# Sums into the output of a Strassen product: from VectorE to ScalarE and an accumulating DMA, with one half of two operand sums emitted two tiles earlier

## The chip, the cores and the metric

The kernel runs on one core of one Trainium2 chip. The metric is the time of one execution on the device in microseconds (us). The core has five engines that work at once, each on its own list of instructions: TensorE (PE; its weight loads are a row of their own, PEld), VectorE (DVE), ScalarE (ACT), GpSimd (POOL) and SyncE (SP). SyncE and GpSimd issue most DMA transfers here. SBUF is the working memory on the chip, PSUM the memory that TensorE writes its results to, DRAM the large memory outside.

## The reference

A decoder trunk of two layers over 512 tokens of width 1024, in float32. Each layer is a mixing part with three attention-like branches, and then a squared-ReLU MLP. The change lies in the MLP alone:

```python
h = rmsnorm(x, norm_mlp_g[l])
x = x + jnp.square(jax.nn.relu(h @ w_up[l])) @ w_down[l]   # w_up 1024 x 4096, w_down 4096 x 1024
```

A last RMSNorm closes the trunk.

## The kernel before, in words

**Number format.** Every float32 operand of a large matmul is split into two parts, `hi` (a ScalarE copy to the matmul's format) and `lo` (what is left, a VectorE subtraction); three matmuls, hi x hi, hi x lo and lo x hi, make one product. `split_to` (L573, L574) does it for activations, `Weights.split` (L159/L160 and L171) for weights, some tiles ahead of their use: four pairs of buffers `whi`/`wlo` stand in a ring, and the code splits two units ahead. The code adds weight blocks for Strassen on VectorE (L438) or by loads whose second DMA adds to the first in SBUF (L123, issued by GpSimd).

**The MLP of a layer.** The 4096 hidden columns are taken in four groups of 1024 (`g` = 0 to 3). For each group eight "up" tiles are computed (`tile_T`, L586 to L588: 24 matmuls of 128 x 512 each). For `g` = 0, 1, 2 the product with `w_down` is one level of Strassen (`strassen()`): hidden and weight matrices are cut 2 x 2, and seven products P1 to P7 take the place of eight. The group `g` = 3 uses the plain product.

**One Strassen product.** `put_h` squares the ReLU of an up tile into the blocks H[t, i, q] (L1500, L1503): t is the half of the tokens, i the half of the hidden columns, q = 0, 1 a tile of 128 x 512 of it. The operands are blocks or sums of blocks: S1 = H11 - H10 (L1531), S2 = S1 - H00 up to sign (L1532), S4 (L1540), and H00 - H10 for P7 (L1525). `split_part` makes the hi and lo of an operand, for q = 0 and 1. `ready_early` makes P1's and P7's operands after the fourth up tile, `ready_sums` S1, S2 and P6's operand after the eighth.

The seven products run in the order P1, P7, P6, P4, P5, P2, P3 (`product`, L1564 to L1566: 24 matmuls each). They sum up in three pairs of PSUM banks: P1, P6, P5, P3 in "B"; P7, P4 in "D"; P2 in "A". After each product its bank's running sum is added to one block of the output (`add_to`), scaled by the token's factor, in tiles `acc[2i + t, j]` in SBUF: eight tiles, 128 x 512 each, that live through `g` = 0, 1, 2. The first sum into a tile is a scaled ScalarE copy (L1584), the others a VectorE instruction that reads PSUM and the tile (L1586):

```python
acc[key] = get()
nc.scalar.activation(acc[key], ps, AF.Copy, scale=r)
...
nc.vector.scalar_tensor_tensor(
    acc[key], in0=ps, scalar=r, in1=acc[key], op0=ALU.mult, op1=ALU.add
)
```

The next product in the same bank, and whoever gets the bank after `give`, has to wait until these have read it. In `g` = 3 `fold` transposes the eight tiles on TensorE (L1642) and adds them to the residual (L1643); the first fold comes with the first up tile of `g` = 3.

**Slots.** Activations, operands and sums share a ring of 42 SBUF tiles of 128 x 512: `get` takes the next free one, `put` gives one back to the end of the line. Whoever writes a slot next waits for its last reader.

**What sets the order.** Work behind a product (sums, splits) is put on a list with `defer` and emitted as soon as the count of emitted TensorE time reaches it, in the order of the calls; `need` and the wait for a free bank emit from that list at once. The order of emission is a priority: a planner (`schedule_with_timeline_sim=True`) then writes each engine's list of instructions, with its own estimates of their times, and takes what it holds to be ready. On the chip each engine follows its list in order. GpSimd's list holds the paired weight loads of the Strassen products (L123), the reload of x (L1377) and its store (L1452).

Of the kernel before, what the change touches and what calls it, by code (L numbers as in the profile page):

```python
# [13 lines left out]
AF = mybir.ActivationFunctionType  # L14
ALU = mybir.AluOpType
# [33 lines left out]
class Weights:  # L49
# [33 lines left out]
    def block(self, kind, srcs):  # L83

        c = len(self.chunks)
        self.chunks.append((srcs, 4, 512))
        self.left.append(None)
        self.queues[kind].append(c)
        return c
# [130 lines left out]
def trunk_kernel(  # L220
# [15 lines left out]
    nc = tc.nc  # L236
# [12 lines left out]
    def get(dtype=F32):  # L249
        i = slots.popleft()  # L250
        t = sb.tile([P, 512], dtype, name=f"slot{i}", tag=f"slot{i}")
        owner[id(t)] = (i, t)
        return t

    def get2():
        return get(R), get(R)

    def put(*ts):
        for t in ts:
            slots.append(owner.pop(id(t))[0])  # L260
# [64 lines left out]
    def defer(fn, delay=0):  # L325
        later.append((clock["t"] + delay, fn))
# [243 lines left out]
    def split_to(hi, lo, src, g=None):  # L570

        if g is None:
            nc.scalar.copy(hi, src)  # L573
            nc.vector.tensor_sub(lo, src, hi.bitcast(F32))  # L574
        else:
            nc.scalar.activation(hi, src, AF.Copy, scale=g)
            nc.vector.scalar_tensor_tensor(lo, in0=src, scalar=g, in1=hi.bitcast(F32), op0=ALU.mult, op1=ALU.subtract)  # L577
# [457 lines left out]
    def layer(l, box):  # L1035
# [381 lines left out]
        scale = {}  # L1417
# [68 lines left out]
        acc = {}  # L1486

        def strassen():

            H, parts = {}, {}  # L1490
# [14 lines left out]

                return go

            def split_part(name, src, free=True):
                got = parts[name] = []
                for q in range(2):  # L1510
                    hi, lo = get2()
                    split_to(hi, lo, src[q])
                    got.append((hi, lo))
                if free:
                    put(*src)

            def block(t, i):
                return [H[t, i, q] for q in range(2)]

            def ready_early():  # L1520

                split_part("P1", block(0, 0), False)
                s = [get() for _ in range(2)]
                for q in range(2):
                    nc.vector.tensor_sub(s[q], H[0, 0, q], H[1, 0, q])  # L1525
                split_part("P7", s)

            def ready_sums():

                for q in range(2):  # L1530
                    nc.vector.tensor_sub(H[1, 0, q], H[1, 1, q], H[1, 0, q])  # L1531
                    nc.vector.scalar_tensor_tensor(  # L1532
                        H[0, 0, q], in0=H[1, 0, q], scalar=-1.0, in1=H[0, 0, q], op0=ALU.mult, op1=ALU.subtract
                    )
                split_part("P6", block(0, 0), False)

            def ready_s4():

# [35 lines left out]
            def add_to(bank, i, j, sign):  # L1574


                def go():
                    for t in range(2):
                        ps = banks[bank][t]
                        r = scale[sign][:, 2 * i + t : 2 * i + t + 1]  # L1580
                        key = (2 * i + t, j)
                        if key not in acc:
                            acc[key] = get()
                            nc.scalar.activation(acc[key], ps, AF.Copy, scale=r)  # L1584
                        else:
                            nc.vector.scalar_tensor_tensor(  # L1586
                                acc[key], in0=ps, scalar=r, in1=acc[key], op0=ALU.mult, op1=ALU.add
                            )

                return go  # L1590

# [6 lines left out]
            for m in range(KD):  # L1598
                yield from tile_T(X, put_h(m))
                if m == 3:  # L1600
                    defer(ready_early)
            defer(ready_sums)
            need("P1", parts)
            yield from product("P1", "B", True, False)
            defer(add_to("B", 0, 0, "+"))
            yield from product("P7", "D", True, False)
            defer(add_to("D", 1, 1, "-"))
            defer(lambda: split_part("P4", block(1, 1)))
            need("P6", parts)
            yield from product("P6", "B", False, False)  # L1610
            defer(add_to("B", 1, 0, "+"))
            defer(lambda: split_part("P5", block(1, 0)))
            need("P4", parts)
            yield from product("P4", "D", False, True)
            defer(add_to("D", 1, 0, "+"))
# [13 lines left out]
            defer(give("B"))  # L1629

        def need(name, parts):
            while name not in parts:
                later.popleft()[1]()

        def fold(m):
# [13 lines left out]
        for g in range(4):  # L1649
            if g < 3:  # L1650
                if g == 2 and l < DEPTH - 1:
                    W.retired.extend(hold["pairs"])
                yield from strassen()
                continue
            for m in range(KD):
                defer(fold(m), 3000 + 4000 * m)
            if l < DEPTH - 1:
                W.retired.append(hold["wide"])
            for m in range(KD):
                yield from tile_T(X, put_up(m))  # L1660
            if (l, g) == (DEPTH - 1, 3):
                for hf in range(2):
                    c = slice(hf * 256, hf * 256 + 256)
                    for m in range(KD):
                        yield from tile_T(Later(hid, KD, c), put_last(m, c))
                    defer(lambda c=c: output(c))
                return
            for m in range(KD):
                yield from tile_T(Later(hid, KD), put_down(m, g == 3))

            def free_h(hs):
                for hi, lo in hs:
                    put(hi, lo)

            hs = [hid.pop(k) for k in range(KD)]
            defer(lambda hs=hs: free_h(hs))
# [80 lines left out]
```

## Time and profile before

| | us |
|---|---|
| three runs | 1826.11 (median), 1825.91, 1828.45 |
| the profiled execution, as timed | 1826.87 |
| its span, first to last instruction | 1825.1 |
| TensorE busy in the span | 1796.6 |
| VectorE busy | 1137.5 |
| ScalarE busy | 806.3 |
| GpSimd busy | 90.9 |

The span is what the trace covers; the time of an execution is 1.8 us longer here. Matmuls are pipelined, so a matmul's row lasts longer than the distance to the next. The lines that the table and the next section are from count times from the start of the span.

### The profile page before, as it was taken

The numbers are of one execution on the slowest core, as the hardware profiler recorded it, in microseconds if no ns is written. First come the engines' busy times: TensorE is split into PE (matmuls) and PEld (weight loads), VectorE is DVE, ScalarE is ACT, GpSimd is POOL, SyncE is SP. The second block draws the span as 40 slices with busy tenths as digits, with TensorE's granted clock in tenths as the row PEclk, the third lists the DMA queues.
The fourth block names the chain that finished last, engine by engine and source line by source line (L and its number), as shares of the span: only waits on it lengthen the run. The fifth ranks groups of instructions, "written<-read, shape, count | busy, mean of one in ns | idle before, by whom it ended". The sixth has DMA issues, their size and how long they took to land.

```text
span 1825.1 us, 22137 instructions
## 1 busy us (share of the span) xinstructions
PE 1796.6 (98%) x8848; PEld 1470.8 (81%) x8848; DVE 1137.5 (62%) x1746; ACT 806.3 (44%) x1359; POOL 90.9 (5%) x105
## 2 busy tenths in 40 slices
PE   7999999999999999999999999999999999999998
PEld 6877777788888887878898777778888888878787
DVE  6785765477454747475648657645765547475756
ACT  5654543133344644443446455422333346445344
POOL 1000000011000101000000000000110001010000
PEclk9999999999999999999999999999999999999999
DMA  6220122135423363623423112222344326362223
GB/s 210 81 93 25 60 93 81 58 95 149 149 92 106 98 179 93 181 65 101 133 78 104 47 37 83 71 92 69 104 139 150 93 92 160 117 163 91 93 93 116
DMA packets 150311, 188.59 MB, mean 103 GB/s; under 512 B 6592, under 2 KB 119760, under 8 KB 150208
## 3 DMA queue, kind: packets, MB, share of 16 engines
q1 hardware_dynamic: 137712, 154.68, 26.5%
q0 software_dynamic: 12352, 32.47, 7.2%
q8 instruction: 69, 1.13, 0.3%
q14 instruction: 34, 0.28, 0.0%
q10 hardware_dynamic: 144, 0.03, 0.0%
HBM read 182.97 MB, written 4.19 MB: 103 GB/s over the span
## 4 chain that ended last, share of the span: by engine, by line
PE 95%; DVE 3%; DMA 1%; ACT 1%; issue 0%; POOLq 0%; SPq 0%; DVEq 0%
PE d L586 12%; PE d L588 12%; PE d L587 12%; PE z L586 8%; PE z L587 8%; PE z L588 8%; PE d L658 3%; PE d L660 3%; PE d L659 3%; PE t L706 3%; PE z L1565 3%; PE z L1566 2%; PE z L1564 2%; PE t L698 2%; PE z L776 2%; PE d L1564 1%
## 5 line engine op out<-in xcount | busy, mean ns | idle before, releaser
L171 ACT CAST whi<-raw 128x1024 fp32r<-128x1024 f32 (+1 forms) x206 | 215.2, 1047 | 393.4 <-PE d L587 132.0
L171 DVE TENSOR_TENSOR wlo<-raw,whi 128x1024 fp32r<-128x1024 f32 (+1 forms) x206 | 249.3, 1212 | 125.5 <-ACT whi L171 106.1
L586 PE MATMUL d<-xh,whi 128*128 128x512 f32 x656 | 262.2, 400 | 8.0 <-ACT whi L171 7.5
L587 PE MATMUL d<-xl,whi 128*128 128x512 f32 x656 | 258.2, 394 | 0.6 <-DVE xl L577 0.6
L588 PE MATMUL d<-xh,wlo 128*128 128x512 f32 x656 | 258.0, 393 | 0.6 <-DVE wlo L171 0.5
L586 PE MATMUL z<-xh,whi 128*128 128x512 f32 x448 | 175.3, 391 | 0.0
L587 PE MATMUL z<-xl,whi 128*128 128x512 f32 x448 | 174.7, 390 | 0.0
L588 PE MATMUL z<-xh,wlo 128*128 128x512 f32 x448 | 173.2, 389 | 0.0
L586 PEld LDWEIGHTS d<-xh,whi 128*128 128x128 f32 x656 | 123.7, 189 | 35.8 <-ACT whi L171 7.9
L588 PEld LDWEIGHTS d<-xh,wlo 128*128 128x128 f32 x656 | 123.6, 188 | 26.8 <-DVE wlo L171 1.7
L587 PEld LDWEIGHTS d<-xl,whi 128*128 128x128 f32 x656 | 123.8, 189 | 26.0 <-DVE xl L577 2.0
L586 PE MATMUL d<-slot,whi 128*128 128x512 f32 (+1 forms) x304 | 121.3, 399 | 0.0
L588 PE MATMUL d<-slot,wlo 128*128 128x512 f32 (+1 forms) x304 | 115.8, 381 | 0.0
L587 PE MATMUL d<-slot,whi 128*128 128x512 f32 (+1 forms) x304 | 115.5, 380 | 0.0
L658 PE MATMUL d<-whi,xh 128*128 128x512 f32 x256 | 102.4, 401 | 0.6 <-ACT slot L1088 0.5
L660 PE MATMUL d<-whi,xl 128*128 128x512 f32 x256 | 100.3, 393 | 0.0
L659 PE MATMUL d<-wlo,xh 128*128 128x512 f32 x256 | 100.0, 391 | 0.0
L588 PEld LDWEIGHTS z<-xh,wlo 128*128 128x128 f32 x448 | 84.1, 188 | 17.6
L586 PEld LDWEIGHTS z<-xh,whi 128*128 128x128 f32 x448 | 84.1, 188 | 17.2
L587 PEld LDWEIGHTS z<-xl,whi 128*128 128x128 f32 x448 | 84.1, 188 | 17.1
L587 PE MATMUL z<-slot,whi 128*128 128x512 f32 (+1 forms) x272 | 95.2, 352 | 0.0
L586 PE MATMUL z<-slot,whi 128*128 128x512 f32 (+1 forms) x272 | 94.8, 352 | 0.0
(268 smaller groups left out, 3525.4 us busy)
## 6 DMA issues: line engine op xcount, KB each, us to landing
raw<-in_w_in_dram SPq DMA_DIRECT2D x53, 1024.0 KB, 5.1
raw<-in_w_down_dram SPq DMA_DIRECT2D x21, 1024.0 KB, 5.1
raw<-in_w_up_dram SPq DMA_DIRECT2D x20, 1024.0 KB, 6.4
work<-in_w_down_dram POOLq DMA_DIRECT2D x36, 512.0 KB, 5.6
aT<-in_w_up_dram SPq DMA_DIRECT2D x12, 1024.0 KB, 5.7
raw<-in_w_branch_dram SPq DMA_DIRECT2D x20, 512.0 KB, 3.5
aT<-in_w_down_dram SPq DMA_DIRECT2D x9, 1024.0 KB, 5.1
extra<-in_w_down_dram POOLq DMA_DIRECT2D x12, 512.0 KB, 8.3
```

The source lines that it names most:

```text
L171: self.last = (nc.scalar.copy(hi, src).ins, nc.vector.tensor_sub(lo, src, hi.bitcast(F32)).ins)
L586: nc.tensor.matmul(ps[:, :w], wh[k], h, start=(k == 0), stop=False)
L587: nc.tensor.matmul(ps[:, :w], wh[k], o, start=False, stop=False)
L588: nc.tensor.matmul(ps[:, :w], wl[k], h, start=False, stop=(k == n - 1))
L658: nc.tensor.matmul(ps[i], h, hi[:, kk], start=(k == 0), stop=False)
L659: nc.tensor.matmul(ps[i], h, lo[:, kk], start=False, stop=False)
L660: nc.tensor.matmul(ps[i], o, hi[:, kk], start=False, stop=(k == KD - 1))
L698: nc.tensor.transpose(ps[:, m * P : (m + 1) * P], a[:, e, j * P : (j + 1) * P], ident)
L706: nc.tensor.matmul(ps[e * 64 : (e + 1) * 64, j * P :], v[j][:, h * 64 : (h + 1) * 64], get_A(e, j), start=(j == 0), stop=(j == NT - 1), sk ...
L776: nc.tensor.matmul(z[:, e, :N], qT[h][:, i * P : (i + 1) * P], kT[h][:, :N], start=True, stop=True)
L1564: nc.tensor.matmul(ps, h, hi[:, kk], start=begin and a, stop=False, skip_group_check=True)
L1565: nc.tensor.matmul(ps, h, lo[:, kk], start=False, stop=False, skip_group_check=True)
```

## The change

Three things are edited. In `add_to` the sum into a tile that exists is no longer one VectorE instruction: ScalarE writes the scaled bank to a fresh slot, a DMA issued by GpSimd adds that slot to the tile of the output in SBUF, and the slot is given back in the code at once. `ready_sums` now makes one half: for q = 0 it is put on the list after the sixth up tile (m = 5), for q = 1 after the eighth (m = 7), where both stood before. `split_part` can split one half alone and gives back its sources one by one, and `need` looks for both halves.

```diff
--- before.py
+++ after.py
@@ -1505,14 +1505,14 @@
 
                 return go
 
-            def split_part(name, src, free=True):
-                got = parts[name] = []
-                for q in range(2):
+            def split_part(name, src, free=True, only=None):
+                got = parts.setdefault(name, [])
+                for q in range(2) if only is None else (only,):
                     hi, lo = get2()
                     split_to(hi, lo, src[q])
                     got.append((hi, lo))
-                if free:
-                    put(*src)
+                    if free:
+                        put(src[q])
 
             def block(t, i):
                 return [H[t, i, q] for q in range(2)]
@@ -1525,14 +1525,13 @@
                     nc.vector.tensor_sub(s[q], H[0, 0, q], H[1, 0, q])
                 split_part("P7", s)
 
-            def ready_sums():
-
-                for q in range(2):
-                    nc.vector.tensor_sub(H[1, 0, q], H[1, 1, q], H[1, 0, q])
-                    nc.vector.scalar_tensor_tensor(
-                        H[0, 0, q], in0=H[1, 0, q], scalar=-1.0, in1=H[0, 0, q], op0=ALU.mult, op1=ALU.subtract
-                    )
-                split_part("P6", block(0, 0), False)
+            def ready_sums(q):
+
+                nc.vector.tensor_sub(H[1, 0, q], H[1, 1, q], H[1, 0, q])
+                nc.vector.scalar_tensor_tensor(
+                    H[0, 0, q], in0=H[1, 0, q], scalar=-1.0, in1=H[0, 0, q], op0=ALU.mult, op1=ALU.subtract
+                )
+                split_part("P6", block(0, 0), False, q)
 
             def ready_s4():
 
@@ -1583,9 +1582,10 @@
                             acc[key] = get()
                             nc.scalar.activation(acc[key], ps, AF.Copy, scale=r)
                         else:
-                            nc.vector.scalar_tensor_tensor(
-                                acc[key], in0=ps, scalar=r, in1=acc[key], op0=ALU.mult, op1=ALU.add
-                            )
+                            a = get()
+                            nc.scalar.activation(a, ps, AF.Copy, scale=r)
+                            nc.gpsimd.dma_start(acc[key], a, accum_op=ALU.add)
+                            put(a)
 
                 return go
 
@@ -1599,7 +1599,8 @@
                 yield from tile_T(X, put_h(m))
                 if m == 3:
                     defer(ready_early)
-            defer(ready_sums)
+                elif m in (5, 7):
+                    defer(lambda q=m % 4 // 2: ready_sums(q))
             need("P1", parts)
             yield from product("P1", "B", True, False)
             defer(add_to("B", 0, 0, "+"))
@@ -1629,7 +1630,7 @@
             defer(give("B"))
 
         def need(name, parts):
-            while name not in parts:
+            while len(parts.get(name, ())) < 2:
                 later.popleft()[1]()
 
         def fold(m):
```

## Rows read from the trace of the kernel before

**Rows 1.** The page's first part: busy us (share of the span) xinstructions.

```profile
PE 1796.6 (98%) x8848; PEld 1470.8 (81%) x8848; DVE 1137.5 (62%) x1746; ACT 806.3 (44%) x1359; POOL 90.9 (5%) x105
```

**Rows 2.** TensorE's waits: who, for whom: us in total, times, longest.

```profile
PE d L1564 <- ACT slot L573: 3.3, 2, 1.7
...
PE d L1564 <- DVE slot L1586: 1.7, 3, 0.8
PE z L1564 <- DVE slot L1586: 1.5, 2, 0.7
...
PE z L1564 <- ACT slot L573: 0.7, 2, 0.3
```

**Rows 3.** First layer's Strassen products: us; PE, PEld, DVE, ACT, POOL busy; clock, DMA.

```profile
612.40:650.80 38.40, 38.40 (x172) 31.79 (x171) 29.99 (x34) 22.00 (x29) 7.77 (x8) 1.00 0.64 166
689.30:740.80 51.50, 49.10 (x210) 39.87 (x209) 40.90 (x49) 23.35 (x35) 7.73 (x8) 0.97 0.51 128
775.20:825.40 50.20, 48.91 (x211) 38.81 (x211) 37.23 (x44) 21.81 (x30) 1.92 (x2) 1.00 0.28 79
```

**Rows 4.** Timeline, second product: start us, us, instruction, count [idle before <-releaser].

```profile
692.30 0.69 DVE L1531 TENSOR_TENSOR slot<-slot,slot 128x512 f32<-128x512 f32 x1
...
701.06 0.73 ACT L1503 ACTIVATE slot<-slot 128x256 f32<-128x256 f32 x2
...
701.70 1.40 DVE L1586 SCALAR_TENSOR_TENSOR slot<-d,rmlp,slot 128x512 f32<-128x512 f32 x2
...
703.02 0.68 DVE L1531 TENSOR_TENSOR slot<-slot,slot 128x512 f32<-128x512 f32 x1
...
704.76 2.49 DVE L574 TENSOR_TENSOR slot<-slot,slot 128x512 fp32r<-128x512 f32 x4
...
707.17 0.68 DVE L1532 SCALAR_TENSOR_TENSOR slot<-slot,slot 128x512 f32<-128x512 f32 x1
...
707.87 1.04 ACT L159 CAST whi<-work 128x1024 fp32r<-128x1024 f32 x1 [1.37 <-PE d L1566]
708.82 0.61 ACT L573 CAST slot<-slot 128x512 fp32r<-128x512 f32 x1
...
709.48 0.73 PE L1564 MATMUL d<-whi,slot 128*128 128x512 f32 x2 [1.65 <-ACT slot L573]
709.51 1.40 DVE L1586 SCALAR_TENSOR_TENSOR slot<-z,nmlp,slot 128x512 f32<-128x512 f32 x2
...
710.96 0.80 PE L1564 MATMUL z<-whi,slot 128*128 128x512 f32 x1 [0.75 <-DVE slot L1586]
```

**Rows 5.** Windows (columns as rows 3) behind that wait, in layers one and two.

```profile
709.50:716.50 7.00, 6.25 (x20) 4.75 (x21) 6.70 (x10) 1.17 (x2) 2.46 (x3) 0.76 0.43 107
1608.40:1615.40 7.00, 6.23 (x25) 4.46 (x25) 7.00 (x10) 1.96 (x2) 2.50 (x3) 1.00 0.43 102
```

**Rows 6.** ScalarE's timeline in the first product and behind it.

```profile
618.41 1.26 ACT L1584 ACTIVATE slot<-z,rmlp 128x512 f32<-128x512 f32 x2
...
651.16 1.05 ACT L171 CAST whi<-aT 128x1024 fp32r<-128x1024 f32 x1 [4.80 <-DMA aT<-in_w_up_dram]
```

**Rows 7.** DMA: GpSimd's queue; issues, KB each, median us to landing.

```profile
q0 software_dynamic: 12352, 32.47, 7.2%
...
work<-in_w_down_dram POOLq DMA_DIRECT2D x36, 512.0 KB, 5.6
...
x_dram<-slot POOLq DMA_DIRECT2D x8, 256.0 KB, 2.4
```

**Rows 8.** GpSimd's timeline in the second product.

```profile
713.14 1.93 POOL L123 DMA_DIRECT2D work<-in_w_down_dram  x2 [3.11 <-DMA work<-in_w_down_dram]
720.48 1.93 POOL L123 DMA_DIRECT2D work<-in_w_down_dram  x2 [5.42 <-DMA work<-in_w_down_dram]
```

**Rows 9.** Timeline, end of the third product and first fold.

```profile
819.95 1.06 ACT L171 CAST whi<-raw 128x1024 fp32r<-128x1024 f32 x1 [5.97 <-PE z L1566]
...
825.20 0.27 PE L1642 MATMUL t<-ident,slot 128*128 128x128 f32 x1
```

## The prediction

> **What bounds the kernel now.** I began with the page's busy times: TensorE is busy for 98% of the span, VectorE for 62%, ScalarE for 44% [rows 1]. TensorE sets the end, so an edit on another engine is worth only what TensorE stops waiting for. The second view is therefore the list of TensorE's waits. The change can touch four lines of it, all at the first matmul of a Strassen step (L1564): 3.3 and 0.7 us until ScalarE's copy of an operand (L573), 1.7 and 1.5 us until VectorE's sum into the output (L1586) [rows 2]. That is 7.2 us, 0.4% of the span, in nine waits; what else TensorE waits for lies outside the Strassen code.
>
> The third view places them: one row for each of the three Strassen products of the first layer [rows 3]. In the first, TensorE is busy for the whole 38.40 us. In the second VectorE is busy for 40.90 of 51.50 us and TensorE misses 2.4; in the third it is 37.23 of 50.20 and 1.3. ScalarE is busy for 23.35 and 21.81 us there. Twice the two losses, for two layers, gives the 7.2 us again within 0.2.
>
> The fourth view, the instructions around one such wait, shows why [rows 4]. The eighth up tile's squares are done at 701.79 (L1503 starts at 701.06 and takes 0.73). The second half of S1 (L1531) waits for VectorE until 703.02, because two sums into the output (L1586, 1.40 us for the pair) stand ahead of it; the second half of S2 (L1532) starts at 707.17, ScalarE's copy of it (L573) at 708.82 behind a weight copy (L159), and TensorE gets P6's second half at 709.48 after 1.65 us of idling. The next pair of sums, from bank "D", starts only at 709.51, and P4, which writes that bank, waits another 0.75 us for it. Behind these two waits the granted clock is 0.76 on the mean over 7 us, between the levels of 2.4 and 1.2 GHz; in the second layer it is 1.00 over the same stretch [rows 5].
>
> **The change part by part.** *The sums.* In a layer the first product makes 3 of its 7 pairs of sums into tiles that exist, the second and third all 7: 17 pairs, 34 instructions, 68 in both layers. VectorE loses 68 x 0.70 us (half of a pair's 1.40) = 48 us. ScalarE gains 68 scaled copies of the form that it already runs for the first sums, 1.26 us for a pair [rows 6]: 68 x 0.63 = 43 us. In the second product, with 14 of each, this brings VectorE from 40.9 to 31 us and ScalarE from 23.4 to 32, of 51.5: neither is full.
>
> GpSimd's queue gains 68 DMA issues of 256 KB. Two issues of 512 KB keep it for 1.93 us [rows 8], so 68 x 0.96 = 65 us over the kernel, on an engine with 90.9 us of work in 1825 [rows 1]. An accumulating DMA between two tiles of SBUF is not in the trace. To its landing I bound it by the plain 256 KB to DRAM, 2.4 us, and the 512 KB of weights on the same queue, most of them accumulating, 5.6 us [rows 7]. The bytes: 68 x 0.262 = 17.8 MB; this queue pays 7.2% of 16 engines' span for 32.47 MB [rows 7], 4.05 us a MB, so together 72 us of all DMA engines. In the first product six of them come among the weight loads, 6.4 us of work. The cover there: the latest weights were copied at 651.16, after ScalarE had waited 4.80 us for them [rows 6], and TensorE did not wait. They are the third up tile's; two tiles of 24 matmuls, 0.227 us apart (10.9 us), run first, from 650.7 to 661.6. I cost this at nothing; without that cover it is up to 6.4 us.
>
> *What it frees.* Without the pair at 701.70, S1's second half can start at 701.8, 1.2 us sooner, and the chain behind it shifts. ScalarE pays 1.26 us for the pair and idles for 1.37 us before 707.87 [rows 4], so its copy at 708.82 need not be later. In the first product the sums after P1 and P7 already are ScalarE copies (618.41 is one) and TensorE never waits there [rows 3, 6]; its tiles run in another order, so this is support, not proof. I count all of the 7.2 us as removed, and with them the clock's 7.0 x 0.24 = 1.7 us: a gain of at most 8.9.
>
> *What it adds.* First, bank D is read by ScalarE. If its pair runs in the idle time before 707.87, P4 waits for nothing; if it runs behind the copy that ends at 709.43, it is done at 710.7 against VectorE's 710.91, and most of the 0.75 stays. Bounds 0 and 0.75; I take 0.4, in the second and third product of both layers: 4 x 0.4 = 1.6 us (0 to 3.0). Second, the last sum into the left half (after P2) is read by the transposes of the first fold. P2 ends at 819.95, the transposes start at 825.20 [rows 9]. ScalarE's pair ends at 821.2, or at 822.3 behind the weight copy that starts at 819.95; 2.4 to 5.6 us later the sum stands, between 823.6 and 827.9. TensorE waits 0 to 2.7 us, once in a layer. The nearer row is the accumulating one, but at twice the bytes: I take 1.0, 2.0 in both layers (0 to 5.4). The Trainium skill (DMA: Bandwidth & Descriptors, "Anatomy of one DMA — SWDGE (gpsimd) path") fits such a DMA as 2.0 us plus bytes over 436 GB/s, an estimated 2.6 us for 256 KB. By it the fold would not wait, and the sum would be 2.0 us lower; the row with accumulating DMAs is longer than that page's fit gives for its bytes (3.2 us), which is why I stay with the rows.
>
> *The halves.* S1's first half already ran at 692.30, 10.7 us before the second [rows 4]: the order on the chip had it early although the code emits both together. Moving its emission two tiles up moves two VectorE steps, one split on ScalarE and VectorE and no DMA; 0, and a gain is not excluded below the 1.65 us counted above. The second half is emitted where it was. Source tiles given back one by one: 0.
>
> **Sum.** The profiled execution took 1826.87 us (span 1825.1, 1.8 around it): 1826.87 - 7.2 - 1.7 + 1.6 + 2.0 = 1821.6. The median of the runs is 1826.11, 0.8 lower, so I predict 1821.0.
>
> **The rivals.**
>
> *ScalarE takes VectorE's place.* It too takes its instructions in a fixed order: a sum written behind a weight copy waits with it, as the copy at 819.95 stood 5.97 us for TensorE [rows 9]. For it: in rows 4 ScalarE has only 0.1 us to spare beyond the new pair. Then P6's wait comes back as L573 behind the sums, some 2 of the 8.9 us stay gained, and the fold takes 2.0: 1826, no change. Against it: 19 us of room in the second product.
>
> *The change does not reach the wait.* P6's copy is late more through the four operand splits (L574 x4, 2.49 us from 704.76) than through the sums. Then 1.3 us go in the second product and 0.8 in the third, 4.2 in both layers, and the fold takes 2.0: 1826.1 - 4.2 + 2.0 = 1823.9.
>
> *Slower: a ScalarE copy waits for an accumulating DMA.* The new DMA reads a slot of the ring of 42. By a count of the takes and returns in the code 10 to 18 slots are free then and a step takes 6, so the slot is written again two or three steps (11 to 16 us) later by an operand split, or sooner where the planner pulls that split ahead. The new DMAs stand in GpSimd's order among the weight loads, and there GpSimd stood 3.11 us and 5.42 us for a load to land [rows 8]. A sum issued behind such a stop lands 5.4 + 5.6 = 11.0 us late; TensorE has two weight units of 12 matmuls (2 x 2.7 us) in hand, so it stops for up to 5.6 us. Loads and sums meet in the first two products of each layer: 4 x 5.6 = 22.4, or 1826.1 - 8.9 + 22.4 = 1839.6. It decides from 3.2 us a product (4 x 3.2 = 12.8 against 8.9). Against it: two or three steps are as long as those 11.0 us. The Trainium skill's same section says that a wait for a semaphore is on the issuing sequencer, before the DMA is dispatched. The trace agrees with those 3.11 and 5.42 us.
>
> **How the numbers follow.** This kernel can tell 0.2% (3.65 us) from no change: faster is below 1822.5, slower above 1829.8. The forecast has 0.46; ScalarE in VectorE's place 0.28; the wait not reached 0.09; the slow case 0.17, of which 0.03 stays under 1829.8. Of the middle cases 0.03 falls below 1822.5: faster 0.49, same 0.37, slower 0.14. The forecast's own range goes from 1826.1 - 8.9 = 1817.2, nothing added, to 1825.6 with both additions at their bounds. I give 1817 to 1829: it takes in that and the middle cases and leaves out the slow case's upper part and a gain beyond the sum, together under 0.2.
>
> **What would show it.** Right: TensorE's waits at L1564 shrink from 7.2 to under 2.5 us, the clock stays at 1.00 behind P6, VectorE loses 48 us and ScalarE gains 43, the new DMAs land within 6 us, and the first fold waits under 2 us. Wrong: ScalarE waits inside the Strassen products for a DMA out of a slot; a first fold held for 3 us or more; L573 or the new copies as what TensorE waits for at P6 or P4, as long as before; or tiles in another order in the second product, which would move the waits for reasons outside this sum.

## The result, and the profile after

The changed kernel takes 1842.81 us (median of 4 runs, 1841.70 to 1849.06), the kernel before beside it 1826.48 us (1825.91 to 1828.45). The ratio is 1.0086, with a 95% interval of 1.0074 to 1.0098: 0.86% slower. The forecast was 1821.0 us with a range of 1817 to 1829, so it was wrong in size and in sign. The profiled execution took 1843.43 us, its span 1841.7; that is 16.6 us more than the span before.

The page of the changed kernel gives the busy times, the row of GpSimd's DMA queue (packets, MB, share of 16 engines) and the DMA issues (count, KB each, median us to landing):

```profile
PE 1802.9 (98%) x8848; PEld 1476.6 (80%) x8848; DVE 1094.5 (59%) x1678; ACT 843.5 (46%) x1427; POOL 149.8 (8%) x173
...
q0 software_dynamic: 22144, 50.30, 12.5%
...
raw<-in_w_up_dram SPq DMA_DIRECT2D x20, 1024.0 KB, 8.8
slot<-slot POOLq DMA_DIRECT2D x68, 256.0 KB, 8.5
```

Against [rows 1] VectorE lost 43 us, ScalarE gained 37 and GpSimd 59, each a little under the forecast's 48, 43 and 65. The queue did not go by the forecast. Its share went from 7.2% [rows 7] to 12.5%: 0.125 x 1841.7 - 0.072 x 1825.1 = 98.8 us of all 16 engines for 68 new DMAs, 1.45 us each, where 72 us had been worked out. They land 8.5 us after their issue, not within 6. The loads of the up projection's weights (w_up) into "raw" land after 8.8 us on the median; in the kernel before it was 6.4.

TensorE's waits in the changed kernel, the first four groups (line waited for: us in total, times, longest us; `z`, `d` and `t` are the names of PSUM tiles, from which the up tiles, the banks A, B and D and the transposes get theirs):

```profile
PE d L586 <- ACT whi L171: 16.5, 5, 6.6
PE z L586 <- ACT slot L1500: 3.0, 2, 2.4
PE t L1643 <- DMA slot<-slot: 2.8, 1, 2.8
PE z L1563 <- ACT whi L159: 2.7, 5, 0.7
```

The lines of [rows 2] are gone: at the Strassen steps (now L1563) 2.7 us are left, for a weight copy. What is new stands at L586, the ordinary up tiles that run between the Strassen products, and at the first fold (L1643). Two waits of the first row stand at the kernel's start (7.2 us; 7.5 before the change). The other three, 9.3 us, and the 3.0 of the second row are new.

Windows place this. First the kernel before, for the stretches that [rows 3] lacks: the two stretches of up tiles between the products in the first layer, then in the second layer up tiles, second product, up tiles, third product (us, length, TensorE's busy time, granted clock, DMA share, GB/s):

```profile
650.71:689.31 38.60, 38.60 (x172) 1.00 0.39 124
740.73:775.25 34.52, 34.52 (x154) 1.00 0.51 166
1549.65:1588.25 38.60, 38.60 (x172) 1.00 0.38 125
1588.25:1638.09 49.84, 47.29 (x204) 1.00 0.54 139
1638.09:1673.74 35.65, 35.65 (x159) 1.00 0.46 151
1673.74:1723.85 50.11, 48.79 (x211) 1.00 0.18 56
```

The changed kernel, by the same stretches: up tiles, second product, up tiles, third product of the first layer, then 7 us from just before the first fold's wait to behind it, then the same four of the second layer:

```profile
650.64:691.92 41.28, 39.47 (x172) 1.00 0.57 164
691.92:741.55 49.63, 48.66 (x212) 1.00 0.72 164
741.55:782.43 40.88, 35.49 (x150) 0.96 0.71 193
782.43:830.99 48.56, 47.88 (x211) 1.00 0.51 106
835.00:842.00 7.00, 6.87 (x27) 0.76 1.05 283
1559.41:1602.22 42.81, 40.40 (x173) 0.96 0.56 158
1602.22:1651.87 49.65, 48.98 (x212) 1.00 0.72 167
1651.87:1692.11 40.24, 37.02 (x151) 0.92 0.72 192
1692.11:1740.66 48.55, 47.87 (x211) 1.00 0.52 110
```

The second and third products became shorter. What TensorE misses in the four of them (length less busy time) was 2.4 and 1.3 us [rows 3], 2.55 and 1.32; now it is 0.97, 0.68, 0.67 and 0.68. That is 4.6 us less, and the second product's clock is 1.00 where it was 0.97. The gain arrived. The four stretches of up tiles had no wait at all; now TensorE waits in them for 1.81, 5.39, 2.41 and 3.22 us, together 12.8, and the clock behind three of the waits takes 0.04 x 40.88 + 0.04 x 42.81 + 0.08 x 40.24 = 6.6 us more. They went from 147.4 to 165.2 us, by 17.8. The first fold adds its 2.8 us of wait and 0.24 x 7.0 = 1.7 us of clock. By waits and clock the balance is 12.8 + 6.6 + 4.5 - 4.6 - 1.7 = 17.6 us, where the spans differ by 16.6; some work changed sides of a boundary, so lengths and waits differ by a microsecond or two.

Which transfer was late shows in the DMA view from 729 to 746 us, the end of the second product. In the kernel before (busy tenths of the DMA engines in 40 slices; two queues; one group of issues with its median time to landing):

```profile
DMA  1001967999999999999999999999999999999999
...
q1 hardware_dynamic: 3069, 3.13, 62.0%
q0 software_dynamic: 555, 1.09, 34.3%
...
raw<-in_w_up_dram SPq DMA_DIRECT2D x2, 1024.0 KB, 10.2
```

and in the changed one:

```profile
DMA  7300294789879999999999999999999999999999
...
q0 software_dynamic: 987, 1.96, 58.8%
q1 hardware_dynamic: 1573, 1.59, 36.2%
...
raw<-in_w_up_dram SPq DMA_DIRECT2D x2, 1024.0 KB, 15.7
slot<-slot POOLq DMA_DIRECT2D x8, 256.0 KB, 13.6
```

The engines were full here already. Eight accumulating DMAs now take a larger part of them; the queue of the weight loads (q1) moved 1.59 MB instead of 3.13 in these 17 us. The Trainium skill (DMA: Bandwidth & Descriptors, "Issuing engines are not separate DMA queues") says that DMAs run on the same 16 engines and interleave, whichever engine issued them. The two queues' shares agree.

The load that TensorE ends up waiting for was issued at 731.3 us before and at 732.0 after. ScalarE's copy of it in the kernel before (start us, us, instruction [idle before <-releaser]):

```profile
745.30 1.05 ACT L171 CAST whi<-raw 128x1024 fp32r<-128x1024 f32 x1 [3.47 <-DMA raw<-in_w_up_dram]
```

ScalarE in the changed kernel:

```profile
741.22 1.26 ACT L1586 ACTIVATE slot<-d,nmlp 128x512 f32<-128x512 f32 x2
742.37 1.04 ACT L171 CAST whi<-raw 128x1024 fp32r<-128x1024 f32 x1
753.09 1.04 ACT L171 CAST whi<-raw 128x1024 fp32r<-128x1024 f32 x1 [9.68 <-DMA raw<-in_w_up_dram]
754.04 0.59 ACT L1500 ACTIVATE slot<-z 128x512 f32<-128x512 f32 x1
```

and TensorE there, at that weight unit and at the first fold:

```profile
754.18 0.80 PE L586 MATMUL d<-xh,whi 128*128 128x512 f32 x1 [5.39 <-ACT whi L171]
...
835.13 0.44 PE L1643 MATMUL t<-ident,slot 128*128 128x128 f32 x2 [2.78 <-DMA slot<-slot]
```

The copy came 7.8 us later than before and TensorE waited 5.39. The rest is the slack that the load had: TensorE was ready at 754.18 - 5.39 = 748.79, the copy takes 1.04, so it was due at 747.7, or 746.9 on the clock of the kernel before, whose stretch begins 0.82 us sooner. There it came at 745.30. The margin was 1.6 us, and nothing of it showed as a wait of TensorE. One more thing stands in these rows: L1500, which empties an up tile's bank "z", came behind the weight copy in ScalarE's order and waited with it. Elsewhere this is what TensorE waits for, in the second group of the waits above: its 2.41 us in the second layer end with an L1500 at 1572.51, behind a weight copy that waited 6.19 us for its load.

The other late load belongs to the place that the prediction looked at, behind the first product [rows 6]. ScalarE's copy of it, TensorE's row that waits for it, and the same matmul in the kernel before:

```profile
656.33 1.05 ACT L171 CAST whi<-aT 128x1024 fp32r<-128x1024 f32 x1 [9.47 <-DMA aT<-in_w_up_dram]
```

```profile
657.43 0.50 PE L586 MATMUL d<-xh,whi 128*128 128x512 f32 x1 [0.67 <-ACT whi L171]
```

```profile
656.67 0.39 PE L586 MATMUL d<-xh,whi 128*128 128x512 f32 x1
```

TensorE's rows have the same order in both kernels: it needs these weights behind 27 matmuls of the stretch, not behind two tiles of 24. In the kernel before, the copy that starts at 651.16 was done 4.5 us ahead of that; in the changed one it came 5.2 us later, so TensorE waited 0.67. The load was issued at 640.56, not at 637.00, and took 15.7 us, not 14.1: 3.6 us of the 5.2 are the later issue (ScalarE's copy that empties the load's buffer stood at 638.23, not at 634.43), 1.6 the longer transfer. The load at the end of the second product was not issued later by the clock of its stretch.

### The profile page after: what moved, and what is told of

Read it like the earlier page. It is cut to its first block, busy times and chain, and to the rows that moved or that the text cites. A ratio compares the mean times of both kernels' runs of the same rounds, so it can differ in the third digit from the quotient of the medians.

```text
span 1841.7 us, 22334 instructions
## 1 busy us (share of the span) xinstructions
PE 1802.9 (98%) x8848; PEld 1476.6 (80%) x8848; DVE 1094.5 (59%) x1678; ACT 843.5 (46%) x1427; POOL 149.8 (8%) x173
## 3 DMA queue, kind: packets, MB, share of 16 engines
q0 software_dynamic: 22144, 50.30, 12.5%
## 4 chain that ended last, share of the span: by engine, by line
PE 77%; issue 14%; DMA 6%; ACT 2%; POOL 1%; DVE 1%; POOLq 0%; SPq 0%; DVEq 0%; ACTq 0%
PE d L586 11%; PE d L588 10%; PE d L587 10%; PE z L588 5%; PE z L586 5%; PE z L587 5%; PE d L658 3%; PE d L660 3%; PE d L659 3%; PE t L706 3%; DMA raw<-in_w_up_dram 2%; PE z L776 2%; PE t L698 2%; DMA slot<-slot 2%; PE z L1565 1%
## 5 line engine op out<-in xcount | busy, mean ns | idle before, releaser
L586 PE MATMUL d<-xh,whi 128*128 128x512 f32 x656 | 264.0, 403 | 16.6 <-ACT whi L171 16.5
L586 PE MATMUL z<-xh,whi 128*128 128x512 f32 x448 | 177.8, 397 | 3.0 <-ACT slot L1500 3.0
L586 PEld LDWEIGHTS d<-xh,whi 128*128 128x128 f32 x656 | 124.3, 189 | 45.4 <-ACT whi L171 18.2
L586 PE MATMUL d<-slot,whi 128*128 128x512 f32 (+1 forms) x304 | 121.3, 399 | 0.0
L586 PEld LDWEIGHTS z<-xh,whi 128*128 128x128 f32 x448 | 85.5, 191 | 21.5 <-ACT slot L1500 3.9
L587 PEld LDWEIGHTS z<-xl,whi 128*128 128x128 f32 x448 | 85.5, 191 | 17.6
L586 PE MATMUL z<-slot,whi 128*128 128x512 f32 (+1 forms) x272 | 94.8, 352 | 0.0
```

What stands on the lines that cost most here:

```text
L586: nc.tensor.matmul(ps[:, :w], wh[k], h, start=(k == 0), stop=False)
L587: nc.tensor.matmul(ps[:, :w], wh[k], o, start=False, stop=False)
```

## The experiments

Three theories. T1: the accumulating DMAs delay the loads of w_up. T2: ScalarE's longer list, in its fixed order, is what makes TensorE wait. T3: the two earlier halves put the tiles or loads in a worse order. The kernel before stood beside each group of runs at 1827.72 (e1 to e4), 1827.92 (e5 to e8) and 1827.13 us (e9 to e11).

**e1_sums_alone.** The kernel before with the new sums and nothing else of the change:

```
-    nc.vector.scalar_tensor_tensor(acc[key], in0=ps, scalar=r, in1=acc[key], ...)
+    a = get()
+    nc.scalar.activation(a, ps, AF.Copy, scale=r)
+    nc.gpsimd.dma_start(acc[key], a, accum_op=ALU.add)
+    put(a)
```

> The sums by ScalarE and an accumulating DMA, the two halves of S1 and S2 emitted together as before. Theory T1 (the new DMAs share the 16 DMA engines with the loads of w_up, which land later, and the up tiles behind the first and second Strassen product wait for weights): 1842 us, within 3, with 15 to 19 us more in the four stretches of up tiles than before. Theory T2 (ScalarE's longer list copies the weights later, their buffers come free later and the loads are issued later; traffic plays no part): the same 1842. Theory T3 (the earlier half gives the planner another order of tiles): 1821 to 1829, the loss gone.

Measured: 1849.45 us, ratio 1.0114 (1.0096 to 1.0133). At L586 TensorE waits 14.2 us for weight copies of ScalarE (7.5 before the change) and 10.9 for L1500, the same kinds as with the whole change. The sums make the loss. But it is 21.7 us here, where the whole change loses 16.3, and the time is above the 1842 within 3 that T1 and T2 expected. Whether the earlier halves save some 5 us beside all the sums is not shown: the two intervals just overlap, and no run looks at it.

**e2_halves_alone.** The other part alone: the changed kernel with the sums on VectorE again, so only P6's halves are emitted apart.

> The earlier half alone, the sums on VectorE as before. T1 and T2: 1826 us, within 2.5, no wait for weights between the Strassen products. T3: over 1835 us.

Measured: 1827.73 us, ratio 1.0001 (0.9991 to 1.0010). The wait for L573 at the Strassen steps is 3.3 us in 2, as in [rows 2]. T3 falls, and the halves alone gain nothing.

**e3_act_then_gpsimd.** ScalarE's instructions as in the change, but no DMA: GpSimd adds the copy in SBUF.

```
-    nc.gpsimd.dma_start(acc[key], a, accum_op=ALU.add)
+    nc.gpsimd.tensor_tensor(acc[key], acc[key], a, op=ALU.add)
```

> As the changed kernel, but GpSimd adds ScalarE's scaled copy to the output tile in SBUF with a tensor add, and no DMA is issued for the sums. T1: the waits of the up tiles for weights and the wait of the first fold go, the 5 us won inside the Strassen products stay: 1820 us, between 1817 and 1824. T2: ScalarE's list is as long as in the changed kernel, so the loads stay late: 1837 to 1843 us. T3: 1837 to 1843 us.

Measured: 1850.87 us, ratio 1.0125 (1.0110 to 1.0140). The total is above what all three theories expected, and a new suspect came in. In the up stretches TensorE's waits are gone but for 0.61 and 0.38 us. The loss is inside the products now, at waits for VectorE's low parts of weights. The groups of VectorE's subtraction and of GpSimd's addition in this run (count | busy, mean ns | idle before), and TensorE's first group of waits:

```profile
L160 DVE TENSOR_TENSOR wlo<-raw,whi 128x1024 fp32r<-128x1024 f32 x24 | 50.2, 2097 | 43.3 <-ACT whi L159 25.6 <-PE z L588 17.7
```

```profile
L1587 POOL TENSOR_TENSOR slot<-slot,slot 128x512 f32<-128x512 f32 x68 | 103.5, 1666 | 253.3 <-ACT slot L1586 253.2
```

```profile
PE d L1564 <- DVE wlo L160: 8.8, 2, 4.4
```

VectorE's subtraction took 2.10 us on the mean; in the changed kernel it took 1.22. The Trainium skill (SBUF — State Buffer, "Who interferes with whom") says that a VectorE instruction with two inputs in SBUF contends with a GpSimd instruction that reads SBUF; the 2.10 us agree. So this run separates T1 from T2 only by place: without the DMAs, ScalarE's list as it fell here cost the up tiles at most 0.6 us in a stretch.

**e4_traffic_alone.** The kernel before, with two plain 256 KB DMAs behind each sum, from a constant to free slots that nobody reads. The sums stay on VectorE and the whole output is computed; the DMAs are work added.

```
+    for e in range(2):
+        q = get()
+        n = nc.gpsimd.dma_start(q, decay[:, e]).ins   # ordered behind the sum
+        put(q)
```

> The kernel before with its sums on VectorE, and behind every such sum two plain DMAs of 256 KB on GpSimd's queue from a constant in SBUF to a free slot, whose content nobody uses: traffic of about the kind and time of the changed kernel's and none of its ScalarE work. T1: the up tiles wait for weights as in the changed kernel, the waits inside the Strassen products stay as before: 1835 to 1850 us, w_up loads up to 15 to 21 us from issue to landing. T2: 1825 to 1829 us, landings as before (14 us at most). T3: 1825 to 1829 us.

Measured: 1858.31 us (one run, so without an interval), 30.6 us slower and 8 above T1's range, with no work added to ScalarE. TensorE's first group of waits in this run, and from its page the queue's row:

```profile
PE z L586 <- ACT whi L171: 21.5, 2, 11.2
```

```profile
q0 software_dynamic: 23232, 68.13, 12.5%
```

Traffic by itself is enough to make the loss at the same place. The share of the queue is the 12.5% of the changed kernel, for 35.7 MB added instead of 17.8: one accumulating DMA keeps the engines about as long as two plain ones of its size.

**e5_early_dma and e6_early2_dma.** Of the changed kernel, only the sums after P1, P7 and P6 (e5), or after P1 and P7 (e6), by ScalarE and the accumulating DMA; the others on VectorE.

```
-    defer(add_to("B", 0, 0, "+"))       # after P1; likewise "D", 1, 1 after P7
+    defer(add_to("B", 0, 0, "+", True)) # True: ScalarE and DMA, else VectorE
```

> The changed kernel, but only the sums after P1, P7 and P6 go by ScalarE and an accumulating DMA; those after P4, P5, P2 and P3 stay on VectorE. The DMAs then run in the first half of a Strassen product, when no load of w_up is on its way. T1 (traffic): no wait of the up tiles for weights, no wait at the first fold, and the waits of P6 and P4 stay away as in the changed kernel: 1821 us against 1826 to 1828 before, between 1818 and 1824. T2 (ScalarE's list makes the loads late): half of its added copies are left, so some of the up tiles' wait stays: 1826 to 1835 us.

> As e5, with the sum after P6 on VectorE too: only those after P1 and P7, which stand in front of P6 and P4, go by ScalarE and DMA. T1: the same 1821 us within 2, since these two are the sums that VectorE made P6 and P4 wait for. T2: 1824 to 1830 us.

Measured: 1821.11 us, ratio 0.9960 (0.9948 to 0.9973), and 1819.19 us, ratio 0.9955 (0.9941 to 0.9969). Both are faster than both kernels; their intervals overlap. Windows of e6, first layer: second product, up tiles, third product (busy times of PE, PEld, DVE, ACT, POOL; clock, DMA):

```profile
689.13:738.24 49.11, 47.71 (x209) 38.86 (x208) 38.26 (x45) 25.48 (x38) 11.25 (x12) 1.00 0.66 158
738.24:772.76 34.52, 34.52 (x155) 28.56 (x153) 16.27 (x19) 17.97 (x31) 0.00 (x0) 1.00 0.52 161
772.76:819.94 47.18, 46.51 (x205) 38.17 (x204) 34.96 (x39) 24.43 (x34) 5.41 (x6) 1.00 0.46 115
```

The up tiles take 34.52 us, as before the change, and the products are 2.3 and 2.9 us shorter than the 51.42 and 50.11 us before (689.31 to 740.73 and 775.25 to 825.36). T1's expectation held for both. The pairs after P1 and P7 are the two that [rows 4] shows in the way, at 701.70 and 709.51. These two pairs, with 16 DMAs early in the products, carry the gain; moving P6's sums too gains nothing more.

**e7_half_dma.** Each pair of sums split: the first by ScalarE and DMA (t == 0), the second by VectorE.

> The changed kernel with one sum of each pair (t = 0) by ScalarE and DMA and the other (t = 1) on VectorE: 34 accumulating DMAs in place of 68. T1: half the added traffic; a load waits only for what is left over its cover, so less than half of the 18 us in the up tiles stays, and part of the gain in the products: 1822 to 1832 us, no w_up load over 16 us from issue to landing. T2: half of ScalarE's added copies: 1828 to 1836 us.

Measured: 1824.18 us, ratio 0.9977 (0.9968 to 0.9986). This is in T1's range and below T2's. With half of the DMAs the up stretches wait 0.39 us at most, although loads of w_up took up to 18.2 us, over the 16 that T1 expected. Half of the traffic does not cost half of the loss; it nearly fits into what the loads have to spare.

**e8_act_then_vector.** ScalarE's instructions as in the change, no DMA, and the addition in SBUF by VectorE.

```
-    nc.gpsimd.dma_start(acc[key], a, accum_op=ALU.add)
+    nc.vector.tensor_add(acc[key], acc[key], a)
```

> The changed kernel, but VectorE adds ScalarE's scaled copy to the output tile in SBUF: ScalarE's list as long as in the changed kernel, no DMA, no GpSimd work. T1: no up tile waits over 1 us for weights; VectorE has as much to do as before, but the bank is read by ScalarE, so P4's wait goes and P6's may stay: 1822 to 1828 us. T2: the loads stay late: 1836 to 1844 us.

Measured: 1838.84 us, ratio 1.0060 (1.0046 to 1.0074): where T2 had put it, against T1. The wait and ScalarE's order around it:

```profile
PE z L586 <- ACT slot L1586: 10.3, 2, 5.2
```

```profile
742.96 1.99 ACT L171 CAST whi<-raw 128x1024 fp32r<-128x1024 f32 x2 [6.44 <-DMA raw<-in_w_up_dram]
744.86 1.26 ACT L1586 ACTIVATE slot<-z,rmlp 128x512 f32<-128x512 f32 x2
```

The load landed 12.0 us after its issue here (13.9 in the kernel before), and TensorE did not wait for its weights. But the new copy out of bank "z" (L1586) stands behind weight copies that wait 6.44 us for that load, and the next up tile needs the bank. In the kernel before VectorE emptied it. So T2's number came out, but not by late loads, as T2 had it: ScalarE's longer list costs TensorE two waits of 5.2 us, one in a layer, without any DMA for the sums. It is not what the changed kernel shows at that place, where the last sum (741.22) is ahead of the late copy (753.09).

**e9_late_dma.** The reverse of e5: the sums after P4, P5, P2 and P3 by ScalarE and DMA, those after P1, P7 and P6 on VectorE.

> The changed kernel with the sums after P1, P7 and P6 back on VectorE; those after P4, P5, P2 and P3 go through ScalarE and the accumulating DMA. Theory (the loss is made by the late sums, in whose time the up projections' weights are loaded; the early sums alone gained 6.8 us): the two are additive, so 1826 + 16.6 + 6.8, about 1850 (1844 to 1856), with the gaps in the two up stretches of each layer and weights of w_up landing over 15 us after their issue. Rival (the DMA engines are only late because the early sums' DMAs are still queued when the late ones come): 1826 to 1838, up stretches within 1 us of before.

Measured: 1858.45 us, ratio 1.0163 (1.0141 to 1.0184). The rival falls; the theory's place is right, but its 1850 is too low by 8 us, and the time is above its range. The rows show both mechanisms, the late load and ScalarE's order; that they make up the whole 8 us is not shown. TensorE's wait in the second stretch of up tiles, then ScalarE:

```profile
756.61 0.80 PE L586 MATMUL z<-xh,whi 128*128 128x512 f32 x1 [7.83 <-ACT whi L171]
```

```profile
755.51 1.04 ACT L171 CAST whi<-raw 128x1024 fp32r<-128x1024 f32 x1 [8.35 <-DMA raw<-in_w_up_dram]
758.30 1.05 ACT L171 CAST whi<-raw 128x1024 fp32r<-128x1024 f32 x1 [1.75 <-DMA raw<-in_w_up_dram]
759.26 1.26 ACT L1586 ACTIVATE slot<-d,nmlp 128x512 f32<-128x512 f32 x2
```

Two loads are late (they took 17.5 and 18.8 us), and a sum out of bank "d" stands behind both copies; in the second layer TensorE waits 6.2 us for such a sum (L1586).

**e10_early2_whole.** e6 without the earlier halves: the kernel before, with the sums after P1 and P7 alone moved.

> The kernel before with the sums after P1 and P7 alone by ScalarE and the accumulating DMA, and P6's operands still made in one piece. Theory (the earlier halves do nothing by themselves): as with the halves, 1818 to 1821. Rival (with the sums off VectorE's list the halves matter, since P6's first operand is then ready sooner): 1822 to 1827.

Measured: 1819.28 us, ratio 0.9954 (0.9937 to 0.9970). This is the theory's range. The halves do nothing here either, so this smallest edit is the version to keep.

**e11_traffic_one.** e4 with one plain DMA behind each sum instead of two (`range(1)`), again work added beside a full computation.

> The kernel before with one plain 256 KB DMA behind each sum, from a constant into a free slot that nobody reads; ScalarE and the sums are as before, and the output is still computed in full. It has half the engine time of the run with two. Theory (the loss goes by the DMA engines' time, in proportion): half of that run's 30 us, 1838 to 1846. Rival (the cost comes only once the queue is full in the second product's end): 1826 to 1833. Either way what the changed kernel loses beyond this run is not bytes but the accumulation's engine time and ScalarE's list.

Measured: 1837.54 us, ratio 1.0054 (1.0039 to 1.0069), 10.4 us slower: just below the theory's range and above the rival's. In the second stretch of up tiles of each layer TensorE waits 3.9 and 1.5 us, both times for L1500 behind a weight copy that waited for its load (8.65 and 7.14 us). The queue's row:

```profile
q0 software_dynamic: 17792, 50.30, 9.8%
```

That is the changed kernel's bytes at 0.098 x 1836.1 - 0.072 x 1825.1 = 48.5 us of engine time, 0.71 us a DMA against 1.45. Half of the engine time that e4 adds costs a third of its loss: the loss grows faster than the traffic, which fits a margin that is used up first.

## Why the prediction was wrong

- **What bounds the kernel, and what the change frees: right, a little large.** The 7.2 us of waits and the 1.7 of clock were to go, less 1.6 for bank D. In the products 4.6 us of waits and the 1.7 went, 6.3 of the net 7.3. Bank D's 1.6 did not come: no wait for the new copies (L1586) is left at a Strassen step. By e6 and e10, 8.7 and 7.9 us faster than the kernel before, two pairs of the seven carry the gain. "I count all of the 7.2 us as removed" was too much; waits for the weight copy L159 took the place of some.
- **The step that failed: the DMAs' cost, "I cost this at nothing; without that cover it is up to 6.4 us".** The cover was looked up at one place, behind the first product, and misread there: the two tiles that were to run first, 10.9 us up to 661.6, were counted by the tiles' numbers. TensorE's rows have 27 matmuls ahead of that weight, up to 656.67, which left 4.5 us behind ScalarE's copy, less than the 6.4 us of DMA work that the prediction had worked out. There TensorE waited 0.67 us for the weight's hi part and 0.53 for its lo part. The end of the second product, with 8 new DMAs, was not looked up at all. There the engines were full before the change and the load had 1.6 us to spare. Together the four stretches of up tiles became 17.8 us longer, where the sum had nothing. e4 and e11 show that traffic alone makes such a loss; e5, e6 and e10, without it at the products' ends, lose nothing there.
- **Its price: too small too.** 4.05 us a MB came from a queue with plain and accumulating transfers mixed; the new ones took 98.8 / 17.8 = 5.5. Even at the forecast's price (72 / 68 = 1.06 us each) the eight DMAs at the second product's end were 8.5 us of engine time against 1.6 us of margin: the place decided, more than the price.
- **The first fold: too small, its total in bounds.** 1.0 us in each layer was taken, 0 to 5.4 in both. 2.78 came in the first layer, none in the second; the clock of 0.76 over 7 us behind it (1.7 us) was not in the sum.
- **The rivals.** "ScalarE takes VectorE's place" named the mechanism of e8, a sum written behind a weight copy, but put it at P6's operand and not at the next up tiles' banks. "The change does not reach the wait" falls: no wait for L573 is left at a Strassen step. The slow rival, a ScalarE copy held by an accumulating DMA's slot, had the right sign for another reason: ScalarE does wait so (L573, 14.2 us in nine waits, the longest 3.7), but the longest wait of TensorE at a Strassen step is 0.7 us.
- **The halves: right at 0**, alone (e2) and beside two pairs of sums (e10); beside all the sums it stays open (e1).

How the loss divides between late loads and ScalarE's order in the changed kernel is shown only as far as its own rows go: of the new waits at L586, 9.3 us end on weight copies and 3.0 on L1500 behind such a copy, and behind the first product most of the load's lateness is its later issue. In e11, which adds nothing to ScalarE, that load was issued at 640.65 too, so the later issue does not need ScalarE's added work. e8 shows an order of ScalarE's same copies that costs 10.3 us without any DMA; e3 that they can also fall in an order that costs the up tiles little. Which of the two orders the changed kernel would take without its DMAs stays open.

## What to carry to other kernels

Work moved from a busy engine to DMA is not free because DMA's mean share is low. Look at the DMA row of the very stretch where each new transfer falls, and work out for each load there how late it may land, from the row of the matmul that first needs it and not from the order in the code; a load that is ready 1.6 us ahead leaves no trace in the list of waits. Then move only the sums that stand in the way: two pairs of the seven gave 0.45%, all of them lost 0.86%. And before an eviction goes to an engine that also copies loaded weights, see which load its place in that order would wait for.

## What the runs showed of the hardware beyond this

- An accumulating DMA of 256 KB between tiles of SBUF took 1.45 us of all 16 DMA engines, a plain one 0.71 (e11). By the same sum it was 1.5 to 1.6 us in e1, e5, e6, e7, e9 and e10.
- With the engines full, the 68 accumulating DMAs landed after 8.5 us on the median; the w_up load behind them took 21.0 us where 13.9 had been the time before.
- GpSimd's addition of two 128x512 fp32 tiles took 1.67 us on the mean, and VectorE's 128x1024 subtraction took 2.10 us in that kernel (e3), 1.22 in the changed one.
